# A two-layer encoder on one core: float32r products of 256 and 258 columns read their moving operand from two runs in turn

## The chip, the core and the metric

The kernel runs on one core of a Trainium2 chip, in one launch. TensorE (PE in the profile; its weight loads are PEld) multiplies, VectorE (DVE), ScalarE (ACT) and GpSimd (POOL) do the rest, and SyncE (SP) issues every DMA. The metric is the device time of a run in microseconds, the median of several runs, and lower is better. Before the change it is 2642.24 us (three runs, 2641.88 to 2644.44).

## The reference

Two layers work on 256 tokens of 2048 features in float32. Each layer has a mixer (two attentions, their gates, an output projection) and a gated FFN with a convolution of width 3 over the tokens; both read a normed input that is scaled and shifted by vectors made from `c`.

```
for l in range(DEPTH):
    mod = c_act @ ada_w[l] + ada_b[l]
    sh_a, sc_a, gt_a, sh_m, sc_m, gt_m = [t[:, None, :] for t in jnp.split(mod, 6, axis=-1)]
    h = rmsnorm(x, norm_mix[l]) * (1.0 + sc_a) + sh_a
    qa, ka, va, qb, kb, vb, ga, gb = split_cols(h @ w_in[l])
    ...
    ya = window_attention(qa, ka, va, sink_a[l]) @ w_proj_a[l]
    yb = neighbourhood_attention(qb, kb, vb, rel_bias_b[l]) @ w_proj_b[l]
    merged = jax.nn.sigmoid(ga) * ya + jax.nn.sigmoid(gb) * yb
    x = x + gt_a * (merged @ w_out[l])
    h = rmsnorm(x, norm_ffn[l]) * (1.0 + sc_m) + sh_m
    u = depthwise_conv(h @ w_up[l], conv_w[l], conv_b[l])
    g, v = jnp.split(u, 2, axis=-1)
    x = x + gt_m * ((jax.nn.silu(g) * v) @ w_down[l])
```

## The kernel before

**Numbers in two halves.** PE multiplies float32r operands. To keep float32's precision, every operand is split into a high part (what float32r keeps) and a low part (the rest), and each product of 128x128 weights with its input becomes three: high by high, high by low, low by high.

**The weight stream.** All weights of a layer stand in one sequence of 128x128 blocks (`block_stream`), 16 blocks to a unit of 1 MB. A DMA brings a unit into `w`; ACT copies each half of it as the high part (line 346) and DVE subtracts it from the original for the low part (line 347), both into a tile `hl`. PE takes the blocks in the order of the sequence. The order of the program is that of the code; a background list (`Paced`) puts the steps of the attention, of the norms and of the modulation vectors (a 2048-long DVE product per vector, line 246) between the units.

**Two kinds of products.** `tokens` (lines 427 to 429, for q, k and v) keeps 128 tokens of `h` as the weights of PE and streams 512 columns of `hl`. It already reads them from two runs of 256 in turn: column 0 of the first run, column 0 of the second, column 1 of the first, and so on. Its result stands in PSUM in the same turn, and its readers take every second column. `features` (through `feature_block`, lines 363 to 365) keeps a block of `hl` as the weights and streams the 256 tokens of one chunk of 128 features: `h`, `merged`, the heads' outputs `oA` and `oB`, or the FFN's activations `act`. It reads them as one run. The two attentions do the same on a smaller scale: lines 673 (scores, in float32r for layer 1) and 711 (values).

**258 columns.** While the norm of `x` is still being made, the first columns of the next matrix are multiplied with the input without its norm (class `Bare`): a chunk holds 256 tokens and two more columns, the high and low part of the shift vector, and `level` (line 588) scales the result afterwards.

**Who reads the results.** Lines 998, 1003 and 451 (gates), 455 (gating), 1050 (residual), 588 (level), 676 (scores), 713 and 714 (values) and 1075 and 1077 (the convolution, which takes tokens with their neighbours) read PSUM columns as they stand. `normed` (lines 518 to 522) writes `h`, for the mixer (w = 0) and the FFN (w = 1) alike.

**Places.** `OFF` and `ROW` (48 and 64 elements) shift tiles against each other: most moving operands of `features` begin 192 bytes after a multiple of 256 bytes as counted from the weights of `hl`; the first chunk of a tile may begin at a multiple of 256.

Of the kernel before, what the change touches and what calls it, by code (L numbers as in the profile page):

```python
# [143 lines left out]
def encoder(ctx: ExitStack, tc: tile.TileContext, a: dict, out: bass.AP):  # L144
# [207 lines left out]
    def unit(l, u):  # L352
# [4 lines left out]
        return halves  # L357

    def feature_block(ps, hl, j, act, first, last):

        hi, lo = hl[:, 0, j * P : (j + 1) * P], hl[:, 1, j * P : (j + 1) * P]
        out = ps[:, : act[0].shape[-1]]
        nc.tensor.matmul(out, hi, act[0], start=first, stop=False)  # L363
        nc.tensor.matmul(ps[:, :S], hi, act[1], start=False, stop=False)  # L364
        nc.tensor.matmul(out, lo, act[0], start=False, stop=last)  # L365

    class Stream:
# [32 lines left out]

        def features(self, acts, evacs, late=None, at={}):
# [12 lines left out]
            for ps, evac in zip(pss, evacs):  # L414
                evac(ps[:, : S if not isinstance(acts[0], tuple) else S + 2])

        def tokens(self, h, kcs):

            pss = [mm.tile([P, 512], F32, name=f"ps{self.l}_{self.u}_t{t}", tag="mm") for t in range(2)]
            for kc in kcs:  # L420
                for _ in range(4):
                    hl, j = self.next_block()
                j -= 3
                hi, lo = (hl[:, i, j * P : (j + 4) * P].rearrange("p (a s) -> p s a", a=2) for i in range(2))
                for t, ps in enumerate(pss):
                    xh, xl = (h[kc][:, i, t * P : (t + 1) * P] for i in range(2))
                    nc.tensor.matmul(ps[:], xh, hi, start=kc == kcs[0], stop=False)  # L427
                    nc.tensor.matmul(ps[:], xh, lo, start=False, stop=False)  # L428
                    nc.tensor.matmul(ps[:], xl, hi, start=False, stop=kc == kcs[-1])  # L429
# [4 lines left out]
            return [ps[:].rearrange("p (s a) -> p a s", a=2) for ps in pss]  # L434

# [76 lines left out]
    def normed(l, w, h, rbs):  # L512

        mod, amod = mods[l], amods[l]
        for kc in range(KC):
# [4 lines left out]
            )  # L520
            nc.scalar.activation(out=h[kc][:, 0], in_=t[:], func=AF.Identity, bias=sh)  # L521
            nc.vector.scalar_tensor_tensor(  # L522
                out=h[kc][:, 1], in0=t[:], scalar=sh, in1=h[kc][:, 0].bitcast(F32), op0=ALU.add, op1=ALU.subtract
            )
# [7 lines left out]
    class Bare:  # L532
# [4 lines left out]
        def __init__(self, l, w, sums):  # L537
# [7 lines left out]
            for tag in homes + ["qn"]:  # L545
# [3 lines left out]
                for i in range(k):  # L549

                    off = 2 * self.half * i + (0 if self.chunks else ROW - OFF)
                    c = t[:, off : off + 2 * self.half].rearrange("p (a s) -> p a s", a=2)
                    self.chunks.append((c[:, 0, : S + 2], c[:, 1, :S]))
            assert len(self.chunks) == KC

        def add(self, kc):
            need(self.l, 48 * self.w + 2 * kc + 2)
            c, scale = self.chunks[kc], amods[self.l][:, self.w, kc : kc + 1]
            sh = mods[self.l][:, 3 * self.w * KC + kc : 3 * self.w * KC + kc + 1]
            hi, lo = c  # L560
            nc.scalar.activation(out=hi[:, :S], in_=x[:, kc], func=AF.Identity, scale=scale)
            nc.vector.scalar_tensor_tensor(
                out=lo, in0=x[:, kc], scalar=scale, in1=hi[:, :S].bitcast(F32), op0=ALU.mult, op1=ALU.subtract
            )
# [18 lines left out]
        def level(self, ps, scale=1.0):  # L583
# [3 lines left out]
            nc.scalar.activation(out=sh[:, 1:], in_=ps[:, S : S + 2], func=AF.Copy, scale=scale, accum_out=sh[:, :1])  # L587
            nc.vector.tensor_tensor(out=z[:], in0=ps[:, :S], in1=self.rbs[:], op=ALU.mult)
            return z, sh
# [78 lines left out]
    def attend(q, k, v, p, mask, scale, sink, o, rows=None):  # L668

        sc = ax.tile([P, 2, S], F32, name="sc", tag="ax")  # L670
        for t in range(2):
            for i, j in by(q):
                nc.tensor.matmul(sc[:, t], q[i][:, t * P : (t + 1) * P], k[j], start=i + j == 0, stop=(i, j) == by(q)[-1])  # L673
        m = sm.tile([P, 2], F32, name="m", tag="m")
        for t in range(2):
            nc.vector.tensor_tensor_reduce(
                out=p[:, t], in0=sc[:, t], in1=mask[:, t], scale=scale, scalar=-3.0e38 if sink is None else sink,
                op0=ALU.add, op1=ALU.max, accum_out=m[:, t : t + 1],
# [30 lines left out]
        for i, j in by(v):  # L709
            for b in range(2):  # L710
                nc.tensor.matmul(po[:, :S], v[i][:, b], pT[:, j, b], start=i + j + b == 0, stop=i + b == 2)  # L711
        o = o()
        nc.scalar.copy(o[:, 0], po[:, :S])
        nc.vector.tensor_tensor(out=o[:, 1], in0=po[:, :S], in1=o[:, 0].bitcast(F32), op=ALU.subtract)

# [120 lines left out]
    for l in range(L):  # L836
# [117 lines left out]
        for pi, (groups, gates) in enumerate(parts):  # L954
# [38 lines left out]
            for mo in range(BARE[0] if l else 0, KC):  # L993

                def gate_a(ps):
                    src = ps
                    if pi > 0:
                        nc.vector.tensor_tensor(out=ya[:, mo], in0=ps, in1=ya[:, mo], op=ALU.add)  # L998
                        src = ya[:, mo]
                    if last:  # L1000
                        half_tanh(ya[:, mo], src)
                    elif pi == 0:
                        nc.scalar.copy(ya[:, mo], ps)

# [6 lines left out]
        for mo in range(KC):  # L1011

            def proj_a(ps):
                gated(ya[:, mo], ya[:, mo], ps)

# [11 lines left out]
        def gate_b(mo):  # L1027
            def evac(ps):
                half_tanh(gb[mo], ps)

# [6 lines left out]
        for mo in range(KC):  # L1037

            def merge(ps):
                z = ev.tile([P, S], F32, name="m", tag="z")  # L1040
                gated(z[:], gb[mo], ps)
                nc.vector.tensor_tensor(out=z[:], in0=z[:], in1=ya[:, mo], op=ALU.add)
# [38 lines left out]
        for gi, chunks in enumerate(FF_GROUPS):  # L1081
# [34 lines left out]
            for cs in sets:  # L1116
# [4 lines left out]
                else:  # L1121
                    for fn in fns:
                        st.features(src, [fn])
                if gi == 0 and cs[-1] == BARE[1] // 2 - 1:
# [107 lines left out]
```

## Time and profile before

| | before |
|---|---|
| median of 3 runs | 2642.24 us |
| the profiled execution, its own time | 2642.45 us |
| its span (first to last instruction) | 2640.7 us |
| granted TensorE clock, mean | 0.999 |
| HBM read, written | 695.06 MB, 2.10 MB |

The span is what the trace covers; 1.75 us lie around it. PE works nearly the whole span. A PE row's length is longer than the distance to the next one, since products overlap in the array: what counts for the time is the distance from start to start, which the lists in order of time and the counts by stretch give.

```profile
PE   8999999999999999999999999999999999999999
DVE  8998998997987888788887778869888776655664
ACT  5445865456643554355555666555575445544553
DMA  9998689885777777777766656677757775555554
```

These are busy tenths in 40 equal slices of 66 us. The products of `tokens` lie in the first five slices (layer 0) and in slices 22 to 24 (layer 1); all the rest is `features` and the attention.

### The profile page before, as it was taken

What the parts mean: (1) busy time and instruction counts of PE and PEld (TensorE: products, weight loads), DVE (VectorE), ACT (ScalarE), POOL (GpSimd) and SP (SyncE); (2) the same over time, 40 slices, a digit from 0 to 9 for tenths busy, and PEclk for the clock granted to TensorE, in tenths of its full rate; (3) what the DMA queues carried; (4) which work ended last, traced back from release to release, by engine and by line L of the source; (5) the groups of instructions that cost most, each with busy time, mean ns of one, the idle gap of its engine ahead of it and who ended that gap; (6) DMA issues with size and microseconds to landing.
All of it is one profiled execution on the core that took longest, in us unless ns stands there. A gap on an engine that the chain in (4) does not pass through costs nothing.

```text
span 2640.7 us, 51000 instructions
## 1 busy us (share of the span) xinstructions
PE 2619.6 (99%) x21164; PEld 2555.7 (97%) x21164; DVE 2120.1 (80%) x2979; ACT 1405.9 (53%) x2280; POOL 247.6 (9%) x345
## 2 busy tenths in 40 slices
PE   8999999999999999999999999999999999999999
PEld 6999899999999999999998889999999999999999
DVE  8998998997987888788887778869888776655664
ACT  5445865456643554355555666555575445544553
POOL 0001100000000000000003658620000000000000
PEclk9999999999999999999999999999999999999999
DMA  9998689885777777777766656677757775555554
GB/s 369 352 348 297 251 316 343 317 326 199 287 288 288 299 291 290 293 288 290 295 224 260 255 210 254 247 269 269 278 181 278 287 262 194 195 199 193 192 192 144
DMA packets 102185, 700.45 MB, mean 265 GB/s; under 512 B 12865, under 2 KB 15169, under 8 KB 18113
## 3 DMA queue, kind: packets, MB, share of 16 engines
q1 hardware_dynamic: 101954, 697.20, 71.1%
q8 instruction: 165, 2.70, 0.4%
q14 instruction: 66, 0.54, 0.1%
HBM read 695.06 MB, written 2.10 MB: 264 GB/s over the span
## 4 chain that ended last, share of the span: by engine, by line
PE 85%; DVE 6%; DMA 3%; POOL 3%; ACT 2%; issue 2%; SPq 0%; POOLq 0%; DVEq 0%; ACTq 0%
PE ps L363 26%; PE ps L365 25%; PE ps L364 25%; PE ps_t L428 2%; PE ps_t L427 2%; PE ps_t L429 2%; DVE hl L347 2%; DMA aw<-in_aw 2%; DVE aw L246 2%; POOL packA L318 1%; POOL p L318 1%; DMA w<-in_ws 1%; ACT hl L346 1%; PE sc L673 1%; PE po L711 1%
## 5 line engine op out<-in xcount | busy, mean ns | idle before, releaser
L347 DVE TENSOR_TENSOR hl<-w,hl 128x1024 fp32r<-128x1024 f32 x928 | 1132.6, 1226 | 325.2 <-ACT hl L346 321.2
L346 ACT CAST hl<-w 128x1024 fp32r<-128x1024 f32 x928 | 969.5, 1049 | 718.9 <-PE ps L365 505.5
L363 PE MATMUL ps<-h,hl 128*128 128x256 f32 x3328 | 922.2, 277 | 1.3 <-DVE ya L998 0.6
L364 PE MATMUL ps<-h,hl 128*128 128x256 f32 x3328 | 919.2, 276 | 0.0
L365 PE MATMUL ps<-h,hl 128*128 128x256 f32 x3328 | 919.0, 276 | 0.0
L363 PEld LDWEIGHTS ps<-h,hl 128*128 128x128 f32 x3328 | 624.7, 188 | 2.4 <-DVE ya L998 0.8
L364 PEld LDWEIGHTS ps<-h,hl 128*128 128x128 f32 x3328 | 624.8, 188 | 0.4 <-DVE h L522 0.2
L365 PEld LDWEIGHTS ps<-h,hl 128*128 128x128 f32 x3328 | 624.3, 188 | 0.0
L246 DVE CUSTOM_DVE_ANT_0 aw<-aw,cact,ab 128x2048 f32<-128x2048 f32 x189 | 443.7, 2348 | 12.3 <-DMA aw<-in_aw 12.2
L427 PE MATMUL ps_t<-hl,h 128*128 128x512 f32 x576 | 217.4, 382 | 4.3 <-ACT h L521 2.7
L1077 DVE SCALAR_TENSOR_TENSOR u<-ps,cw,u 128x255 f32<-128x255 f32 x304 | 146.2, 481 | 92.9 <-ACT u L1075 88.5
L428 PE MATMUL ps_t<-hl,h 128*128 128x512 f32 x576 | 219.6, 382 | 1.1 <-DVE hl L347 0.9
L429 PE MATMUL ps_t<-hl,h 128*128 128x512 f32 x576 | 218.6, 380 | 0.0
L1075 ACT ACTIVATE u<-ps,cw 128x256 f32<-128x256 f32 x152 | 85.7, 564 | 214.8 <-PE ps L365 214.7
L365 PE MATMUL ps<-merged,hl 128*128 128x256 f32 x512 | 141.7, 277 | 0.5 <-DVE hl L347 0.5
L364 PE MATMUL ps<-merged,hl 128*128 128x256 f32 x512 | 141.5, 277 | 0.0
L363 PE MATMUL ps<-merged,hl 128*128 128x256 f32 x512 | 141.5, 277 | 0.0
L364 PE MATMUL ps<-act_o,hl 128*128 128x256 f32 x512 | 141.3, 276 | 0.0
L365 PE MATMUL ps<-act_o,hl 128*128 128x256 f32 x512 | 141.3, 276 | 0.0
L363 PE MATMUL ps<-act_o,hl 128*128 128x256 f32 x512 | 141.0, 276 | 0.0
L427 PEld LDWEIGHTS ps_t<-hl,h 128*128 128x128 f32 x576 | 108.9, 190 | 20.9 <-ACT h L521 3.7
L428 PEld LDWEIGHTS ps_t<-hl,h 128*128 128x128 f32 x576 | 109.2, 190 | 18.1 <-DVE hl L347 3.2
(244 smaller groups left out, 4817.1 us busy)
## 6 DMA issues: line engine op xcount, KB each, us to landing
w<-in_ws SPq DMA_DIRECT2D x463, 1024.0 KB, 4.9
aw<-in_aw SPq DMA_DIRECT2D x189, 1024.0 KB, 5.5
p<-in_bias SPq DMA_DIRECT2D x16, 256.0 KB, 4.5
x<-in_xT SPq DMA_DIRECT2D x4, 512.0 KB, 5.5
aw_o<-in_aw SPq DMA_DIRECT2D x2, 1024.0 KB, 12.4
out<-x SPq DMA_DIRECT2D x16, 128.0 KB, 2.5
w<-in_ws SPq DMA_DIRECT2D x2, 512.0 KB, 11.7
aw_b<-in_aw SPq DMA_DIRECT2D x1, 1024.0 KB, 18.2
```

The costliest lines, as they stand in the source:

```text
L246: product = nc.vector.tensor_tensor_reduce(out=raw[:], in0=raw[:], in1=cact[:], scale=1.0, scalar=ab[:, i : i + 1], op0=ALU.mult, op1=ALU. ...
L318: nc.gpsimd.tensor_copy(out=dst[a : a + BLOCK, :, :, b : b + BLOCK], in_=src[b : b + BLOCK, :, :, a : a + BLOCK])
L346: nc.scalar.copy(hl[:, 0], r)
L347: nc.vector.tensor_tensor(out=hl[:, 1], in0=r, in1=hl[:, 0].bitcast(F32), op=ALU.subtract)
L363: nc.tensor.matmul(out, hi, act[0], start=first, stop=False)
L364: nc.tensor.matmul(ps[:, :S], hi, act[1], start=False, stop=False)
L365: nc.tensor.matmul(out, lo, act[0], start=False, stop=last)
L427: nc.tensor.matmul(ps[:], xh, hi, start=kc == kcs[0], stop=False)
L428: nc.tensor.matmul(ps[:], xh, lo, start=False, stop=False)
L429: nc.tensor.matmul(ps[:], xl, hi, start=False, stop=kc == kcs[-1])
L1075: nc.scalar.activation(out=u, in_=ps, func=AF.Identity, scale=w[:, 1:2], bias=w[:, 3:4])
L1077: nc.vector.scalar_tensor_tensor(out=u[:, to], in0=ps[:, of], scalar=w[:, j : j + 1], in1=u[:, to], op0=ALU.mult, op1=ALU.add)
```

## The change

All float32r products of 256 and 258 columns now read the moving operand from two runs in turn, as `tokens` did: columns 0, 128, 1, 129 and so on (0, 129, 1, 130 with 258). The number of columns, of products and of weight loads stays, and each product still writes its columns of PSUM one after another, so PSUM holds tokens 0, 128, 1, 129. Readers take every second column, and write two runs of 128. A chunk of 258 puts the two columns of the shift behind each run. The FFN's `h` is stored turned instead (even tokens in the first run, odd ones in the second), so that its product comes out in the order of the tokens and the convolution reads PSUM as before (`sorted=True`). The float32 scores of layer 0 (one term, `len(q) == 1`) stay as they were.

```
+    def turns(columns):
+        return columns.rearrange("p (r q) -> p q r", r=2)
+    def turned_back(columns):
+        return columns.rearrange("p (q r) -> p r q", r=2)
+    def pair(columns):
+        return columns.rearrange("p (r q) -> p r q", r=2)
...
     def feature_block(ps, hl, j, act, first, last):
-        out = ps[:, : act[0].shape[-1]]
+        out = ps[:, : 2 * act[0].shape[1]]
...
-                    feature_block(ps, hl, j, (act[:, 0], act[:, 1]) if not isinstance(act, tuple) else act, i == 0, i == len(acts) - 1)
+                    act_of = act if isinstance(act, tuple) else (turns(act[:, 0]), turns(act[:, 1]))
+                    feature_block(ps, hl, j, act_of, i == 0, i == len(acts) - 1)
...
-                evac(ps[:, : S if not isinstance(acts[0], tuple) else S + 2])
+                evac(ps[:, : S + 2] if isinstance(acts[0], tuple) else ps[:, :S] if sorted else turned_back(ps[:, :S]))
...
+            hi, lo, src = h[kc][:, 0], h[kc][:, 1], t[:]
+            if w:
+                hi, lo, src = turns(hi), turns(lo), src.rearrange("p (q r) -> p q r", r=2)
-            nc.scalar.activation(out=h[kc][:, 0], in_=t[:], func=AF.Identity, bias=sh)
+            nc.scalar.activation(out=hi, in_=src, func=AF.Identity, bias=sh)
...
-                    self.chunks.append((c[:, 0, : S + 2], c[:, 1, :S]))
+                    self.chunks.append((turns(c[:, 0, : S + 2]), turns(c[:, 1, :S])))
...
-            nc.scalar.copy(hi[:, S : S + 1], sh)
-            nc.vector.tensor_tensor(out=hi[:, S + 1 :], in0=sh, in1=hi[:, S : S + 1].bitcast(F32), op=ALU.subtract)
+            src, first, second = pair(x[:, kc]), hi[:, 0, P:], hi[:, 1, P:]
+            nc.scalar.copy(first, sh)
+            nc.vector.tensor_tensor(out=second, in0=sh, in1=first.bitcast(F32), op=ALU.subtract)
...
-                nc.tensor.matmul(po[:, :S], v[i][:, b], pT[:, j, b], start=i + j + b == 0, stop=i + b == 2)
+                nc.tensor.matmul(po[:, :S], v[i][:, b], turns(pT[:, j, b]), start=i + j + b == 0, stop=i + b == 2)
...
-            nc.vector.scalar_tensor_tensor(out=x[:, mo], in0=ps, scalar=gt, in1=x[:, mo], op0=ALU.mult, op1=ALU.add)
+            to = pair(x[:, mo])
+            nc.vector.scalar_tensor_tensor(out=to, in0=ps, scalar=gt, in1=to, op0=ALU.mult, op1=ALU.add)
```

PE, POOL and SP keep their instructions in the same order, and every tile keeps its address. 109 more waits stand on PE, each for one of its own products that lies at least 20 products back. On ACT and DVE one thing moves: the copies of the shift (128x1) for the last chunks of a `Bare` set now stand behind the chunk's own write instead of up to a dozen units ahead of it. First ACT, at the end of layer 0's output projection (`bare_1_y` are chunks of the FFN's unnormed input, `hl_99` and `hl_100` weight units). Before:

```order
L561 ACTIVATE bare_1_y_5621<-x,amod_177 128x256
L346 CAST hl_99_0_6635<-w_99_6633 128x1024
L346 CAST hl_99_1_6638<-w_99_6633 128x1024
L473 ACTIVATE sq<-x 128x256
L561 ACTIVATE bare_1_y_5622<-x,amod_177 128x256
L346 CAST hl_100_0_6643<-w_100_6641 128x1024
```

and after, at the same place:

```order
L578 ACTIVATE bare_1_y_5621<-x,amod_177 128x2x128
L346 CAST hl_99_0_6635<-w_99_6633 128x1024
L582 CAST bare_1_y_5621<-mod_172 128x1
L346 CAST hl_99_1_6638<-w_99_6633 128x1024
L486 ACTIVATE sq<-x 128x256
L578 ACTIVATE bare_1_y_5622<-x,amod_177 128x2x128
L346 CAST hl_100_0_6643<-w_100_6641 128x1024
L582 CAST bare_1_y_5622<-mod_172 128x1
```

The 128x1 copy of each chunk now comes one weight copy after the chunk. On DVE at the same place, where the second shift column is made, before:

```order
L562 SCALAR_TENSOR_TENSOR bare_1_y_5621<-x,amod_177,bare_1_y_5621 128x256
L347 TENSOR_TENSOR hl_99_0_6635<-w_99_6633,hl_99_0_6635 128x1024
L1050 SCALAR_TENSOR_TENSOR x<-ps_97_16_0_6499,mod_172,x 128x256
L347 TENSOR_TENSOR hl_99_1_6638<-w_99_6633,hl_99_1_6638 128x1024
L475 TENSOR_TENSOR sqa<-sqa,sq 128x256
```

and after:

```order
L579 SCALAR_TENSOR_TENSOR bare_1_y_5621<-x,amod_177,bare_1_y_5621 128x256
L347 TENSOR_TENSOR hl_99_0_6635<-w_99_6633,hl_99_0_6635 128x1024
L583 TENSOR_TENSOR bare_1_y_5621<-mod_172,bare_1_y_5621 128x1
L1071 SCALAR_TENSOR_TENSOR x<-ps_97_16_0_6499,mod_172,x 128x256
L347 TENSOR_TENSOR hl_99_1_6638<-w_99_6633,hl_99_1_6638 128x1024
```

Here too one 128x1 subtraction has moved in ahead of the residual's read of PSUM.

More of the change, by code (lines that the diff above doesn't have):

```diff
@@ L399, in next_block, with features @@
             return self.halves[j // 8], j % 8
-        def features(self, acts, evacs, late=None, at={}):
+        def features(self, acts, evacs, late=None, at={}, sorted=False):
             pss = [mm.tile([P, 512], F32, name=f"ps{self.l}_{self.u}_{self.at}_{m}", tag="mm") for m in range(len(evacs))]
@@ L423, in tokens @@
                 j -= 3
-                hi, lo = (hl[:, i, j * P : (j + 4) * P].rearrange("p (a s) -> p s a", a=2) for i in range(2))
+                hi, lo = (turns(hl[:, i, j * P : (j + 4) * P]) for i in range(2))
                 for t, ps in enumerate(pss):
@@ L433, in tokens @@
                     self.tick()
-            return [ps[:].rearrange("p (s a) -> p a s", a=2) for ps in pss]
+            return [turned_back(ps[:]) for ps in pss]
     def split(dst, src, scale=None, held=False):
@@ L587, in level @@
             nc.scalar.activation(out=sh[:, 1:], in_=ps[:, S : S + 2], func=AF.Copy, scale=scale, accum_out=sh[:, :1])
[L588 removed]
+            nc.vector.tensor_tensor(out=pair(z[:]), in0=turned_back(ps[:, :S]), in1=pair(self.rbs[:]), op=ALU.mult)
             return z, sh
@@ L672, in attend @@
             for i, j in by(q):
-                nc.tensor.matmul(sc[:, t], q[i][:, t * P : (t + 1) * P], k[j], start=i + j == 0, stop=(i, j) == by(q)[-1])
+                key = turns(k[j]) if len(q) > 1 else k[j]
+                nc.tensor.matmul(sc[:, t], q[i][:, t * P : (t + 1) * P], key, start=i + j == 0, stop=(i, j) == by(q)[-1])
         m = sm.tile([P, 2], F32, name="m", tag="m")
@@ L1122, in encoder @@
                     for fn in fns:
-                        st.features(src, [fn])
+                        st.features(src, [fn], sorted=True)
                 if gi == 0 and cs[-1] == BARE[1] // 2 - 1:
```

32 lines of the change are left out of this document (17 added, 15 removed).

## The prediction

> **What bounds the kernel now.** I read the page first: its busy times, then its chain of work that ended last.
>
> ```profile
> PE 2619.6 (99%) x21164; PEld 2555.7 (97%) x21164; DVE 2120.1 (80%) x2979; ACT 1405.9 (53%) x2280; POOL 247.6 (9%) x345
> PE 85%; DVE 6%; DMA 3%; POOL 3%; ACT 2%; issue 2%; SPq 0%; POOLq 0%; DVEq 0%; ACTq 0%
> PE ps L363 26%; PE ps L365 25%; PE ps L364 25%; PE ps_t L428 2%; PE ps_t L427 2%; PE ps_t L429 2%; DVE hl L347 2%; DMA aw<-in_aw 2%; DVE aw L246 2%; POOL packA L318 1%; POOL p L318 1%; DMA w<-in_ws 1%; ACT hl L346 1%; PE sc L673 1%; PE po L711 1%
> ```
>
> Three lines of PE, those of `feature_block`, hold 76% of the chain. Next I looked where other engines set the end, in a table by stretches (us, then the busy time of PE, PEld, DVE, ACT, POOL with their instructions, the granted clock, the DMA share, GB/s):
>
> ```profile
> 0.00:330.00 330.00, 317.19 (x1860) 281.41 (x1861) 301.04 (x431) 187.33 (x363) 22.24 (x15) 1.00 0.86 324
> 330.00:396.00 66.00, 66.00 (x540) 64.30 (x540) 63.68 (x119) 40.83 (x85) 0.00 (x0) 1.00 0.85 316
> 396.00:1385.00 989.00, 988.53 (x8630) 987.28 (x8630) 840.71 (x1155) 513.65 (x775) 2.32 (x2) 1.00 0.77 288
> 1385.00:1600.00 215.00, 210.53 (x1051) 186.13 (x1051) 159.03 (x233) 129.82 (x279) 120.16 (x167) 0.98 0.65 245
> 1600.00:2636.00 1036.00, 1036.00 (x9080) 1035.48 (x9080) 755.19 (x1042) 534.22 (x782) 102.91 (x161) 1.00 0.62 227
> ```
>
> The third and the fifth stretch are nearly all products of 256 and 258 columns, and PE has no gap: 989 us for 8630 products is 114.6 ns each, 1036 us for 9080 is 114.1 ns. The clock is granted in full, so neither waits nor throttling explain the pace. Up to 330 us and around 1500 us lie the 512-column products; at 330 to 396 us DVE works 63.68 of 66 us and PE needs 122 ns for an instruction, so DVE sets the pace there.
>
> What is one product's pace made of? Lists in order of time, first and last row of each group (start, length, line): 55 rows of 256 columns in one run, 34 rows of 512 columns in two runs, 53 rows of `Bare`, mixed 258 and 256.
>
> ```profile
> 1079.77 0.28 PE L365 MATMUL ps<-act_b,hl 128*128 128x256 f32 x1
> ...
> 1085.89 0.28 PE L365 MATMUL ps<-act_b,hl 128*128 128x256 f32 x1
> ```
> ```profile
> 1463.78 0.38 PE L428 MATMUL ps_t<-hl,h 128*128 128x512 f32 x1
> ...
> 1470.90 0.38 PE L428 MATMUL ps_t<-hl,h 128*128 128x512 f32 x1
> ```
> ```profile
> 1929.77 0.28 PE L365 MATMUL ps<-bare_b,hl 128*128 128x258 f32 x1
> ...
> 1935.95 0.28 PE L363 MATMUL ps<-bare_qn,hl 128*128 128x258 f32 x1
> ```
>
> From start to start: 6.12 us over 54 steps, 113.3 ns; 7.12 over 33, 215.8 ns; 6.18 over 52, 118.8 ns. Half of 215.8 is 107.9 ns: columns that come from two runs stream faster than one run of 256, though the two-run products have a weight load beside them too. With two more columns the pace falls by 5.5 ns, far more than two columns' share, 0.8 ns. So the one-run stream loses time to something that depends on timing, and I take it for a clash of its reads with those of the weight load. A run of 256 columns covers 1024 bytes in the time in which the load covers 512, so it overtakes the load; two runs of 128 walk 512 bytes each, at the load's own pace. That is my reading; no row shows a clash itself.
>
> The other bound is the weight load. [...]
>
> ```profile
> 13.54 2.76 PEld L462 LDWEIGHTS warm<-ident 128*128 128x128 f32 x24
> 619.08 0.19 PEld L365 LDWEIGHTS ps<-bare_a,hl 128*128 128x128 f32 x1
> ...
> 619.19 0.19 PEld L363 LDWEIGHTS ps<-bare_a,hl 128*128 128x128 f32 x1
> ```
>
> 24 loads of the warming products (4-byte weights, 128 columns) take 2.76 us, less the last one's 0.19: 2.57 over 23 steps, 111.7 ns. The float32r load at 619.08, which follows a product of one column and has no long stream beside it, is followed by the next after 0.11 us. So loads one behind the other need about 111.7 ns, whatever streams.
>
> **The change part by part.** *The reading.* It removes no product; it changes the pace of 6272 + 6272 + 6272 (lines 363 to 365), 192 (line 711) and 96 (line 673), 19,104 in all. From below the new pace is bound by half the two-run product, 107.9 ns, and by the load's 111.7 ns; from above by the present mixed pace of 118.8 ns, should a clash remain. I take **111.7 ns**, the nearest row, since it has the same load beside a stream that covers 512 bytes in a product, as each run will. Does the load itself survive beside two runs?
>
> ```profile
> L428 PEld LDWEIGHTS ps_t<-hl,h 128*128 128x128 f32 x576 | 109.2, 190 | 18.1 <-DVE hl L347 3.2
> L364 PEld LDWEIGHTS ps<-h,hl 128*128 128x128 f32 x3328 | 624.8, 188 | 0.4 <-DVE h L522 0.2
> L482 PEld LDWEIGHTS ssm<-mean,sq 128*128 128x128 f32 x8 | 1.1, 192 | 0.0
> ```
>
> Beside a two-run stream it lasts 190 ns, beside one run 188, beside a product of one column 192: the two runs don't stretch it.
>
> The sum by stretches: 989 - 8630 x 0.1117 = 25.0 us and 1036 - 9080 x 0.1117 = 21.8 us, together **47 us**. The few transposes and score products in these counts are priced alike, a small error. From the 1,600 or so further one-run products (before 396 us and around 1500 us) I count nothing: DVE and the DMAs are late next there (DMA share 0.86 up to 330 us). If they gained as much, 2.6 ns each, it would be 4 us. In the two long stretches DVE, 840.71 us in 989, would go to 87% of the shorter time and the DMA share from 0.77 to 0.79: neither becomes the bound on average.
>
> A rule of the Trainium skill speaks against this. In "SBUF — State Buffer", section "Door 1: The DMA port swizzle", it says that accesses which stay in a 16-byte line get the full bandwidth and that each one which crosses to a new line pays; with two runs in turn every column is in another line than the last. The trace gives no sign of such a price at 512 columns, where two runs take 215.8 ns, less than twice 113.3; a row of 512 float32r columns in one run is not there to compare. What it would do to the time stands with the last rival.
>
> *The readers.* Readers of PSUM with every second column are in the trace already, next to plain ones:
>
> ```profile
> L968 DVE TENSOR_TENSOR packB<-ps_t,packB 128x512 f32<-128x512 f32 x24 | 15.7, 681 | 0.0
> L998 DVE TENSOR_TENSOR ya<-ps,ya 128x256 f32<-128x256 f32 x32 | 13.0, 416 | 3.4 <-PE ps L365 3.4
> L966 ACT COPY packB<-ps_t 128x512 f32<-128x512 f32 x12 | 6.7, 585 | 5.4 <-PE ps_t L429 5.2
> L1003 ACT COPY ya<-ps 128x256 f32<-128x256 f32 x16 | 5.8, 370 | 12.2 <-PE ps L365 12.2
> L347 DVE TENSOR_TENSOR hl<-w,hl 128x1024 fp32r<-128x1024 f32 x928 | 1132.6, 1226 | 325.2 <-ACT hl L346 321.2
> L346 ACT CAST hl<-w 128x1024 fp32r<-128x1024 f32 x928 | 969.5, 1049 | 718.9 <-PE ps L365 505.5
> ```
>
> From a plain read of 256 columns to one of 512 with the stride DVE needs 265 ns more (1.04 a column), from 256 to the 1024 plain columns of line 347 810 ns more (1.05). ACT's steps are 215 ns (0.84) and 679 (0.88). So the stride has no price: 0, and in the long stretches both engines have idle time that would hide a small one.
>
> *The FFN's `h`, stored turned.* 32 writes on ACT and 32 on DVE put neighbours 512 bytes apart. No row shows that. Bounds: nothing, or as much again as the whole instruction, 479 ns on DVE (line 522): 32 x 0.48 = 15 us, half for each layer, in a stretch where DVE has about a seventh of its time free and the first products that need this `h` come only after the `Bare` set. I take 0; uncovered it would be up to 15 us.
>
> *What moves.* Nine pairs of 128x1 copies stand later on ACT and DVE, and nothing is removed or doubled; the chunks they complete are read by PE after more weight units. Cost 0; three pairs in a row at the end, uncovered, are under 1 us. *The new waits.* PE's 109 waits are for its own products 20 or more back, which is over 2 us ago: always met. Behind a waiting product stands the rest of PE, but it would not stop.
>
> The sum stands against the profiled execution's own time, 2642.45 us, 0.2 us above the median 2642.24: 2642.45 - 47 = 2595.4, so **2595 us**.
>
> **The rivals.**
>
> *The load hides and the stream alone counts.* For it: float32r loads show 188 to 190 ns against the 192 of float32's, so their own pace may lie below 111.7. Against: the step of 0.11 us after one-column products. Midway between 107.9 and 111.7, at 109.8 ns, 989 - 947.6 and 1036 - 997.0 give 80 us: 2562; at 107.9 it is 114 us, 2528. "TensorE: Matmul & The Clock Gate" in the Trainium skill (section "Back-to-back issue gap") has columns / 2.4 + 2.5 ns, thus 109.2 ns for 256, and that would be an estimate of 2551; at 512 columns its 215.8 is what the trace has.
>
> *The pace stays.* 113.3 ns would be what a float32r load needs beside any stream, or the change doesn't touch what slows the stream. For it: 113.3 is only 1.6 above the loads' own pace. Then at best the irregular products come down to it: 989 - 978.0 and 1036 - 1029.0 make 18 us, 2624; or nothing, 2642.
>
> *Slower: the turn costs more line reads.* Each column then opens another place in the memory than the column before, and a load that shares the pace of both runs may meet them all the time instead of in passing, above all where first chunks lie at the weights' own offset. It decides in every `features` product, from a mean pace above the present 114.3 ns. Priced at the irregular pace of today, 118.8 ns: 17,710 products x 118.8 = 2104 us against 2025, 79 us more, 2721. Against it: the three load rows and the 512-column pace. At its worst each column costs double. The nearest row for that is the float32 score product, whose rows of 256 columns last as long as those of 512 float32r columns:
>
> ```profile
> 1463.99 0.38 PE L429 MATMUL ps_t<-hl,h 128*128 128x512 f32 x1
> L673 PE MATMUL sc<-packA 128*128 128x256 f32 x32 | 9.4, 380 | 0.0
> ```
>
> Both last 380 ns, so I price it at the 512 columns' pace: 17,710 x (215.8 - 114.3) adds 1.8 ms. The line rule of the Trainium skill cited above is of this kind, without a figure. I give that end 0.02 of the chance of slower.
>
> **How the numbers follow.** The forecast (a pace of 110.8 to 112.5, 2580 to 2612 us) 0.58; the stream alone 0.13; the pace stays 0.14, of which 0.05 with a gain that can be told; slower 0.15. Faster is 0.58 + 0.13 + 0.05 = 0.76, same 0.09, slower 0.15; 0.2%, some 5 us, is about what a measurement of this kernel can tell from no change. The range leaves out the slower rival and the end of the second: 2540 to 2645.
>
> **What would show it.** The stretches of plain products should hold 590 or 591 products in 66 us (583 to 585 now), and the products of `Bare` should keep the same pace as the others, no longer 118.8. The matmul rows of 256 columns should last some 274 ns instead of 276. Unchanged DVE and ACT means at lines 1050, 455 and 451 would bear out the readers. A pace that stays at 113.3 in the long stretches, longer load rows than 192 ns, or a DVE that is busy without gaps while PE waits would each prove a step wrong.

## The result, and the profile after

The changed kernel takes 2605.79 us, the median of four runs (2603.60 to 2608.11), beside 2642.14 us for the kernel before in four runs. The ratio is 0.9861 with a 95% interval of 0.9844 to 0.9878: 36 us faster, where 47 had been forecast (2595 us). Its profiled execution took 2603.6 us, the lowest of the four, with a span of 2601.8 us: 38.9 us less than the span of before.

The page of the kernel after, first the busy times and then the chain of work that ended last, by engine and by line:

```profile
PE 2574.4 (99%) x21164; PEld 2507.9 (96%) x21164; DVE 2122.7 (82%) x2979; ACT 1404.2 (54%) x2280; POOL 247.9 (10%) x345
PE 78%; DVE 9%; DMA 4%; ACT 3%; POOL 3%; issue 3%; SPq 0%; DVEq 0%; POOLq 0%; ACTq 0%
PE ps L377 23%; PE ps L375 23%; PE ps L376 23%; DVE hl L347 3%; DMA aw<-in_aw 3%; PE ps_t L440 2%; PE ps_t L441 2%; PE ps_t L442 2%; DVE aw L246 2%; ACT hl L346 1%; POOL packA L318 1%; POOL p L318 1%; DMA w<-in_ws 1%; PE sc L691 1%; POOL qrs L506 1%
```

DVE's work is nearly the same (2120.1 us before), but PE's share of the chain has fallen from 85% to 78%, and DVE's and the DMAs' have grown from 9% to 13% together. PE is still busy 99% of the span, yet it now waits for others in places where it did not. The table by stretches of the kernel after has the same products in each row as that of before (the borders are the starts of the same products; columns as there):

```profile
0.00:329.20 329.20, 316.31 (x1860) 280.05 (x1861) 301.13 (x431) 187.25 (x363) 22.25 (x15) 0.99 0.86 324
329.20:393.80 64.60, 64.48 (x541) 62.51 (x541) 62.07 (x119) 39.24 (x81) 0.00 (x0) 1.00 0.84 315
393.80:1365.10 971.30, 967.79 (x8631) 965.13 (x8630) 843.77 (x1155) 514.30 (x778) 2.32 (x2) 1.00 0.79 294
1365.10:1579.30 214.20, 209.25 (x1051) 184.86 (x1050) 159.02 (x233) 129.51 (x279) 120.37 (x167) 0.99 0.66 246
1579.30:2595.70 1016.40, 1015.33 (x9081) 1014.26 (x9081) 756.23 (x1042) 533.92 (x783) 102.94 (x161) 1.00 0.64 231
```

Row by row, against before: 0.8 us less, 1.4 less, **17.7 less** (forecast 25.0), 0.8 less, **19.6 less** (forecast 21.8). Behind the last row 6.1 us are left, where before had 4.7: 1.4 us more. Together that is the 38.9 us.

The pace itself is in the lists in order of time: first and last row of 55 plain products of 256 columns, and of 58 products of `Bare`, both of the kernel after.

```profile
1060.80 0.28 PE L375 MATMUL ps<-act_b,hl 128*128 128x256 f32 x1
...
1066.83 0.28 PE L375 MATMUL ps<-act_b,hl 128*128 128x256 f32 x1
...
1901.95 0.27 PE L376 MATMUL ps<-bare_b,hl 128*128 128x256 f32 x1
...
1908.32 0.27 PE L376 MATMUL ps<-bare_qn,hl 128*128 128x256 f32 x1
```

6.03 us over 54 steps are 111.7 ns, and 6.37 us over 57 steps are 111.8 ns: plain products and `Bare` now have the same pace, that of the load. The groups of lines 375 and 376 say the same in another way:

```profile
L375 PE MATMUL ps<-h,hl 128*128 128x256 f32 x3328 | 916.1, 275 | 1.9 <-DVE ri L709 0.8
L376 PEld LDWEIGHTS ps<-h,hl 128*128 128x128 f32 x3328 | 638.9, 192 | 0.4 <-DVE h L538 0.2
```

A product lasts 275 ns (277 at this place before), a load 192 instead of 188: no longer than beside a product of one column (192). A window of 66 us, in the FFN of layer 1, of before and then of after (counts include the rows that lap over an edge):

```profile
2400.00:2466.00 66.00, 66.00 (x583) 66.00 (x582) 39.91 (x49) 31.39 (x39) 0.00 (x0) 1.00 0.54 192
```
```profile
2400.00:2466.00 66.00, 66.00 (x593) 66.00 (x592) 45.89 (x63) 35.38 (x50) 0.00 (x0) 1.00 0.55 193
```

Readers of every second column of PSUM, in the kernel after:

```profile
L1018 DVE TENSOR_TENSOR ya<-ps,ya 128x256 f32<-128x256 f32 x32 | 13.0, 417 | 2.6 <-PE ps L377 2.6
L1023 ACT COPY ya<-ps 128x256 f32<-128x256 f32 x16 | 5.8, 370 | 11.5 <-PE ps L377 11.5
L1071 DVE SCALAR_TENSOR_TENSOR x<-ps,mod,x 128x256 f32<-128x256 f32 x128 | 60.0, 479 | 19.7 <-PE ps L377 19.2
```

With the columns read in a row these had 416, 370 and 478 ns. The stride costs a reader nothing.

The writers of the FFN's `h`, stored turned, are another matter. Length of one (smallest, median, largest ns) on DVE in layer 0, before and then after, and last on ACT after:

```profile
L522 DVE SCALAR_TENSOR_TENSOR h<-ht,mod,h x16: 478/482/486, 629.1 to 679.5; 128x256 fp32r<-128x256 f32 x16
```
```profile
L538 DVE SCALAR_TENSOR_TENSOR h<-ht,mod,h x16: 667/690/709, 623.9 to 674.7; 128x256 fp32r<-128x256 f32 x16
```
```profile
L537 ACT ACTIVATE h<-ht,mod x16: 713/752/776, 623.1 to 673.2; 128x256 fp32r<-128x256 f32 x16
```

For 256 columns with neighbours 512 bytes apart DVE needs 208 ns more; its instruction also reads one operand, the high part, in that order. ACT only writes so. The group of all its 64 writes, before and then after:

```profile
L521 ACT ACTIVATE h<-ht,mod 128x256 fp32r<-128x256 f32 x64 | 30.4, 501 | 32.1 <-DVE ht L518 31.8
```
```profile
L537 ACT ACTIVATE h<-ht,mod 128x256 fp32r<-128x256 f32 x64 | 37.2, 626 | 33.9 <-DVE ht L531 33.5
```

Half of them are turned: about 250 ns more for each turned write. By length that is 6.7 us more on DVE (32 x 0.208) and 8.0 on ACT. Neighbouring rows overlap a little: by busy time the groups grew by 6.8 us on ACT (30.4 to 37.2) and by 6.2 on DVE (29.5 to 35.7). The turned writes lie in the stretch of `Bare` (610 to 680 us, and again in layer 1).

### The profile page after: what moved, and what is told of

It is laid out like the page before. It is cut to its first block, busy times and chain, and to the rows that moved or that the text cites. A ratio compares the mean times of both kernels' runs of the same rounds, so it can differ in the third digit from the quotient of the medians.

```text
span 2601.8 us, 51007 instructions
## 1 busy us (share of the span) xinstructions
PE 2574.4 (99%) x21164; PEld 2507.9 (96%) x21164; DVE 2122.7 (82%) x2979; ACT 1404.2 (54%) x2280; POOL 247.9 (10%) x345
## 4 chain that ended last, share of the span: by engine, by line
PE 78%; DVE 9%; DMA 4%; ACT 3%; POOL 3%; issue 3%; SPq 0%; DVEq 0%; POOLq 0%; ACTq 0%
PE ps L377 23%; PE ps L375 23%; PE ps L376 23%; DVE hl L347 3%; DMA aw<-in_aw 3%; PE ps_t L440 2%; PE ps_t L441 2%; PE ps_t L442 2%; DVE aw L246 2%; ACT hl L346 1%; POOL packA L318 1%; POOL p L318 1%; DMA w<-in_ws 1%; PE sc L691 1%; POOL qrs L506 1%
## 5 line engine op out<-in xcount | busy, mean ns | idle before, releaser
L375 PEld LDWEIGHTS ps<-h,hl 128*128 128x128 f32 x3328 | 638.8, 192 | 3.1 <-ACT hl L346 0.9
L376 PEld LDWEIGHTS ps<-h,hl 128*128 128x128 f32 x3328 | 638.9, 192 | 0.4 <-DVE h L538 0.2
L377 PEld LDWEIGHTS ps<-h,hl 128*128 128x128 f32 x3328 | 638.6, 192 | 0.0
L246 DVE CUSTOM_DVE_ANT_0 aw<-aw,cact,ab 128x2048 f32<-128x2048 f32 x189 | 444.0, 2350 | 12.1 <-DMA aw<-in_aw 11.7
L1096 ACT ACTIVATE u<-ps,cw 128x256 f32<-128x256 f32 x152 | 85.8, 564 | 198.6 <-PE ps L377 198.6
```

The source lines that it names most:

```text
L246: product = nc.vector.tensor_tensor_reduce(out=raw[:], in0=raw[:], in1=cact[:], scale=1.0, scalar=ab[:, i : i + 1], op0=ALU.mult, op1=ALU. ...
L1096: nc.scalar.activation(out=u, in_=ps, func=AF.Identity, scale=w[:, 1:2], bias=w[:, 3:4])
```

## The experiments

Two questions were open: what makes the pace 111.7 ns with two runs and more with one, and who took the missing 10 us.

**Shorter streams.** In after (`narrow_two`) and in before (`narrow_one`, as one run) the second and third product of each block read 192 of their columns. The edit in after:

```
+NARROW = 192
...
-        nc.tensor.matmul(ps[:, :S], hi, act[1], start=False, stop=False)
-        nc.tensor.matmul(out, lo, act[0], start=False, stop=last)
+        nc.tensor.matmul(ps[:, :NARROW], hi, act[1][:, : NARROW // 2], start=False, stop=False)
+        nc.tensor.matmul(ps[:, :NARROW], lo, act[0][:, : NARROW // 2], start=False, stop=last)
```

> The changed kernel with the second and third product of each block of features cut from 256 (258) to 192 columns; it leaves out the two correcting products for 64 of the 256 tokens. Theory L (loading weights, 111.7 ns each, sets the new pace): the pace stays at 111.7 ns, 590 to 592 products in 66 us, time 2600 to 2610 us. Rival S (the stream sets it): two of three products shrink to three quarters, near 84 ns, the mean to 93, and some 300 us go, until VectorE is the bound: 2250 to 2350 us.

> The kernel before with the same cut to 192 columns, read as one run; it leaves out the two correcting products for 64 of the 256 tokens. Theory C1 (beside a weight load the one-run stream is stretched, the load itself is not): the narrow products have room to spare and take the load's 111.7 ns, the 256-column ones keep 113 to 119; mean near 112.5 ns, time 2605 to 2618 us. Rival C2 (the load is stretched by the stream): all products stay at 113.3 ns or more, 2628 to 2645 us.

Measured: 2910.76 and 2938.82 us. Both times are far above every expectation, but the pace can be read where PE doesn't wait. PE's rows of `narrow_two` in order of time:

```profile
2400.13 0.25 PE L377 MATMUL ps<-act_o,hl 128*128 128x192 f32 x1
2400.21 0.28 PE L378 MATMUL ps<-act_o,hl 128*128 128x192 f32 x1
2400.32 0.30 PE L376 MATMUL ps<-act_o,hl 128*128 128x256 f32 x1
2400.46 0.25 PE L377 MATMUL ps<-act_o,hl 128*128 128x192 f32 x1
```

The steps differ, but three products take 0.33 us, as many as with 256 columns (3 x 111.7 = 335 ns): a sixth of the columns is gone and not a nanosecond is won. So the weight load sets the pace of after, and the shorter streams gained nothing here.

A window of 66 us from 2400 us on holds 594 products in `narrow_two`. In `narrow_one` it is

```profile
2400.00:2466.00 66.00, 66.00 (x584) 66.00 (x584) 48.78 (x53) 28.12 (x31) 0.00 (x0) 1.00 0.76 288
```

The products that start there are 113.4 ns apart on average, and three take 340 ns, 5 more than in two runs. So one run keeps the extra of all three products, though two of them have 64 columns to spare. The mean is that of theory C2 (the load is stretched), but 4 of the 5 ns lie in the step behind the 256-column product, as C1 has it. Whether the stream or the load is stretched stays open.

The times rose for another reason. What DVE waited for, and a window in layer 0, of `narrow_two`:

```profile
DVE aw L247 <- DMA aw<-in_aw: 238.3, 65, 6.8
```
```profile
540.00:612.00 72.00, 47.71 (x316) 46.26 (x315) 33.13 (x43) 21.62 (x35) 0.00 (x0) 0.74 0.52 194
```

DVE waits 238 us for the loads of the modulation vectors (11.7 us idle for that reason in after), PE stands a third of the window, and its granted clock is 0.74 there. With narrower products the order of the work on ACT, DVE and SP is not that of after either, so these two times say nothing on the change; the circle behind such waits comes up again below.

**Other ways to turn.** In two kernels made from after, `features` reads its 256 columns from four runs of 64 in turn (`four_runs`), or the even columns and then the odd ones (`evens_odds`).

```
...
-                    act_of = act if isinstance(act, tuple) else (turns(act[:, 0]), turns(act[:, 1]))
+                    act_of = act if isinstance(act, tuple) else tuple(act[:, i].rearrange("p (r q) -> p q r", r=4) for i in range(2))
```
```
...
+                    act_of = act if isinstance(act, tuple) else tuple(act[:, i].rearrange("p (q r) -> p r q", r=2) for i in range(2))
```

> The changed kernel, but products of 256 columns read four runs of 64 in turn, and their results come out with the tokens in another order (readers are not adapted). Theory P (a clash is avoided because each run walks through the memory at the load's own pace): four runs walk at half the load's pace, which passes them, so the pace is irregular again, 113 to 119 ns, 2630 to 2720 us. Rival R (taking columns from far places in turn is enough): 111.7 ns, 2600 to 2610 us.

> The changed kernel, but products of 256 columns read all even columns of one run and then all odd ones (readers are not adapted, tokens come out in another order). Theory P: the stream walks four times as fast as the load and passes it twice, so the pace is that of before or worse, 113 to 119 ns, 2635 to 2720 us. Rival R needs places far apart in turn and expects 113.3 ns as well, 2635 to 2645 us. Rival Q (fewer of the columns of a 16-byte piece in a row is what helps): 111.7 ns, 2600 to 2610 us.

Measured: 3133.98 and 4623.3 us. Windows of 66 us without a wait, of `four_runs` and then of `evens_odds`:

```profile
2700.00:2766.00 66.00, 66.00 (x464) 66.00 (x463) 32.63 (x42) 26.32 (x34) 0.00 (x0) 1.00 0.45 160
```
```profile
4000.00:4066.00 66.00, 66.00 (x290) 59.80 (x289) 18.60 (x21) 13.31 (x14) 0.00 (x0) 1.00 0.28 96
```

From start to start it is 143 and 229 ns: no theory had such sizes. Neither kernel is held by the load's pace (111.7 ns); the stream itself is slower. In "SBUF — State Buffer" of the Trainium skill, section "Door 1: The DMA port swizzle", two hits in each 16-byte line are enough for the full bandwidth and a new line for each access pays. Here every second column in a row, which hits each line twice, takes twice as long (229 ns). Two runs in turn, which change the line with every column, pay nothing (111.7 ns), while four, which change it as often, do pay (143 ns). So these runs don't bear the rule out for this stream.

**How near the two runs lie.** `four_runs` differs from after in the number of runs and in their distance, 256 bytes instead of 512. `two_near` has two runs at 256 bytes:

```
...
+                    act_of = act if isinstance(act, tuple) else tuple(act[:, i].rearrange("p (h r q) -> p h q r", h=2, r=2) for i in range(2))
```

> After's feature products read two runs in turn that begin 256 bytes apart (each half of 128 columns as two runs of 64 in turn) in place of 512 bytes apart; the Bare and token products stay as in after. The columns arrive in another order than their readers take, so the output isn't the reference's. What made the run with four runs of 64 columns take 143 ns per product? Theory N (number of runs: a third and fourth run cost, two are free at any distance): 111.7 ns, 2600 to 2610 us. Theory D (distance: 256 bytes is too near): 125 to 145 ns, 2820 to 3140 us.

Measured: 2602.01 us in one run, and the window has as many products as after's:

```profile
2400.00:2466.00 66.00, 66.00 (x594) 66.00 (x592) 45.88 (x63) 35.38 (x50) 0.00 (x0) 1.00 0.55 193
```

Theory N: whether two runs lie 256 or 512 bytes apart doesn't matter; that there are four does.

**Where the operands lie.** The pads between the tiles taken out of after (`flat_two`) and of before (`flat_one`), so that moving operand and weights begin at the same place:

```
-OFF, ROW = 48, 64
+OFF, ROW = 0, 0
```

> After's kernel with the two pads taken out of the activations' places (OFF and ROW 0 in place of 48 and 64 words), so that nearly every moving operand begins at the same place, modulo 1 KB, as the weights. The sums are unchanged and so is the order of the instructions on every engine. Theory P (two runs meet no clash, whatever their place): pace 111.7 ns as in after, 2600 to 2610 us. Rival (the gain of two runs needs these places too): 113 to 120 ns per product, 2630 to 2760 us.

> Before's kernel with the same two pads taken out: one run, at the weights' own place. Theory P (one run clashes with the load's reads, by its place): the pace of all products becomes that of the one chunk that lies so in before (113 to 119 ns, mean near 116): 19,100 products by 2 to 3.5 ns more than 114.1, so 2675 to 2710 us. Rival (the place doesn't matter, one run is slow by itself): 114.1 ns and 2642 us as before.

Measured: 2603.86 us for two runs, 2749.22 us for one. The same window, `flat_two` and then `flat_one`:

```profile
2400.00:2466.00 66.00, 66.00 (x593) 66.00 (x593) 45.88 (x63) 35.55 (x49) 0.00 (x0) 1.00 0.54 196
```
```profile
2400.00:2466.00 66.00, 66.00 (x552) 66.00 (x551) 36.84 (x46) 27.71 (x33) 0.00 (x0) 1.00 0.52 178
```

Two runs keep 111.6 ns (mean of the 19,013 steps up to 160 ns behind products of 256 and 258 columns); one run goes from 114.2 to 119.9 ns, all over the kernel, with nothing changed but addresses. So how long a one-run product takes depends on where its operands lie, and a two-run product shows no such dependence. Theory P holds, though its price was low (119.9 instead of 116). The edit shifts operands and weights against each other and also in memory as a whole; which of the two counts wasn't separated.

**One run of 512 columns.** In after, `tokens` alone goes back to one run.

```
-                hi, lo = (turns(hl[:, i, j * P : (j + 4) * P]) for i in range(2))
+                hi, lo = (hl[:, i, j * P : (j + 4) * P] for i in range(2))
...
-            return [turned_back(ps[:]) for ps in pss]
+            return [pair(ps[:]) for ps in pss]
```

> After's kernel with the token products (1,728 of 512 columns, at 215.9 ns in before and after, which both read two runs in turn) put back to one run; its readers take the columns plainly. Theory C (one run clashes only while a weight load of 128 columns runs beside it): 4 ns more per product at most, as the 256-column product lost (113.3 ns against its 109 of stream): 218 to 220 ns, 2608 to 2614 us by 1,700 of them where waits don't take it. Rival R (a one-run stream is slower over its whole length): twice that per product, 222 to 226 ns, 2615 to 2623 us. Rival 0 (512 columns hide it): 215.9 ns, no change.

Measured: 2609.41 us. First and last of 37 rows of `tokens_one`:

```profile
1439.64 0.39 PE L442 MATMUL ps_t<-hl,h 128*128 128x512 f32 x1
...
1447.80 0.39 PE L442 MATMUL ps_t<-hl,h 128*128 128x512 f32 x1
```

8.16 us over 36 steps are 226.7 ns; the mean of all 1,679 steps up to 250 ns is 228.1, against 215.9 in two runs: 12.2 ns for each product, more than either theory had. The time, 5.6 us above that of `flat_two`, would fit theory C, but it can't decide: it is one run, runs of after alone lie between 2600 and 2609 us, and of the 20.5 us that 1,679 x 12.2 ns would make, most is hidden where `tokens` waits anyway.

By the kernel's addresses, nine in ten of these products (1566 of 1728) have moving operand and weights at the same place modulo 256 bytes, as in `flat_one`, where one run of 256 columns lost 119.9 - 107.9 = 12.0 ns on half of 215.8. There the 512-column product loses as much, once and not twice, which would speak for C's mechanism. The other tenth, 192 bytes apart like most products of 256 columns in before, speaks against it. Six of them in a row in `tokens_one` start with the first of these rows and end where the second starts:

```profile
1458.22 0.40 PE L440 MATMUL ps_t<-hl,h 128*128 128x512 f32 x1
...
1459.62 0.39 PE L440 MATMUL ps_t<-hl,h 128*128 128x512 f32 x1
```

1.40 us over six steps are 233 ns, 17 more than in two runs. A product of 256 columns lost 113.3 - 107.9 = 5.4 ns at that place. So here twice the length loses three times as much, and the place that is the better one for 256 columns is the worse one for 512. Neither C nor R holds as stated; how the loss goes with length and place stays open.

**DVE's work in the out-projection of layer 0.** In after this stretch was no shorter than before (88.4 and 88.6 us), with DVE busy for 92% of it. Before and then after:

```profile
527.30:615.70 88.40, 87.94 (x770) 87.75 (x769) 80.19 (x125) 46.01 (x77) 0.00 (x0) 1.00 0.85 315
```
```profile
522.20:610.80 88.60, 86.86 (x771) 86.10 (x770) 81.85 (x128) 46.47 (x77) 0.00 (x0) 1.00 0.86 315
```

Three kernels side by side: after itself (`after_again`), 30 additions given to POOL (`pool_adds`), the same 30 left out (`no_adds`). The edits of the second are

```
+             self.eng = nc.gpsimd if name == "ssm0" else nc.vector
-                nc.vector.tensor_tensor(out=self.acc[:], in0=self.acc[:], in1=sq[:], op=ALU.add)
+                self.eng.tensor_tensor(out=self.acc[:], in0=self.acc[:], in1=sq[:], op=ALU.add)
...
-                nc.vector.tensor_tensor(out=z[:], in0=z[:], in1=ya[:, mo], op=ALU.add)
+                (nc.vector if l else nc.gpsimd).tensor_tensor(out=z[:], in0=z[:], in1=ya[:, mo], op=ALU.add)
```

and the third has these two statements under a condition that leaves layer 0 out.

> After's kernel unchanged, as the measure for the two runs beside it: 2602 to 2609 us.

> After's kernel with 30 additions of 128x256 in layer 0 (the 16 that add the branches' merge, the 14 that add up squares behind the out-projection; 0.42 us each on DVE) given from DVE to POOL, which has 0.70 us of work between 522 and 680 us. Theory W (in these 158 us of after's profile DVE is 90% busy and late, so that the faster pace gives nothing there): some 12 us of DVE's work less, PE waits 2 to 3 us less, 2600 to 2604 us where the unchanged kernel of the same call has 2605. Rival (the weights' DMA or ACT ends last there, or POOL is too slow to hand the sums over in time): no change within 0.1%, or 2 to 5 us more.

> After's kernel with the same 30 additions of layer 0 left out altogether (so its output isn't the reference's): the most that giving them away can bring. Theory W: 2599 to 2603 us, 2 to 6 less than the unchanged kernel. Rival (DVE isn't what is late): the same as the unchanged kernel within 2 us.

Measured: 2604.62 us (ratio to before 0.9839 to 0.9872), 2617.99 us (0.9893 to 0.9923) and 2604.94 us (0.9839 to 0.9868). Theory W falls: without the additions nothing is won. The four runs of each kernel spread over 6 to 8 us, so the times alone could not tell the 2 us that W had at least; but the stretch itself is no shorter either, 90.1 us beside 89.8 in `after_again`. The stretch of `no_adds`, and what DVE waits for most in it:

```profile
522.00:612.10 90.10, 87.27 (x771) 86.19 (x770) 74.64 (x105) 45.85 (x76) 0.00 (x0) 1.00 0.84 308
```
```profile
DVE aw L246 <- DMA aw<-in_aw: 8.8, 7, 2.4
```

In the same stretch of `after_again` DVE waits 4.2 us for these loads. DVE has some 7 us less to do (74.64 us beside 81.97) and spends more than half of it on waiting for the loads of the modulation vectors. Its rows show the circle. Chain of waits of `no_adds` between 562 and 582 us (start, us, what; the first row is the share by line):

```profile
by line: DMA aw<-in_aw 59.8%; issue 33.2%; DVE hl L347 11.4%; DVE bare_b L580 2.0%; DVE x L1073 2.0%; DVE mod L246 1.4%; DVE aw L246 0.4%; DVE amod L255 0.3%; DVEq L347 0.1%
...
562.29 4.84 DMA aw<-in_aw
...
569.54 7.11 DMA aw<-in_aw
```

The load at 562.29 is issued 0.02 us after DVE's product of the vector before, which frees one of the four 1 MB buffers; it lands 4.84 us later, and DVE takes it at once. The next, at 569.54, again follows that product and takes 7.11 us. Splits of weights (line 347) stand behind these products on DVE. A DVE with less to do waits longer for the next load (8.8 us beside 4.2).

`pool_adds` is worse for a reason of its own: POOL needs 1.26 us for one such addition where DVE needs 0.42, and PE waits for the merge. Groups of POOL and waits of PE in its out-projection stretch:

```profile
L489 POOL TENSOR_TENSOR sqa<-sqa,sq 128x256 f32<-128x256 f32 x13 | 16.3, 1257 | 59.5 <-ACT sq L487 59.4
```
```profile
PE ps L375 <- DVE m L468: 5.2, 2, 2.8
```

**Fewer loads.** After without 16 of the modulation vectors of layer 0:

```
+LEFT_OUT = range(64, 80)
...
         for n, i in enumerate(ADA_ORDER):
+            if l == 0 and n in LEFT_OUT:
+                nc.vector.memset(mod[:, i : i + 1], 1.0)
...
+                done[l] = n + 1
+                yield
+                continue
```

> After's kernel without 16 of the modulation vectors of layer 0 (numbers 64 to 79 in their order: their 1 MB loads, which share four buffers with the weight units, and DVE's product of 2.35 us each; the values are set to 1 instead, so the output isn't the reference's). In no_adds DVE's extra free time went into waiting for these loads: each is issued when DVE frees a buffer, lands 5 to 7 us later, and DVE's next split of weights stands behind it. Theory B (that circle of load, DVE and buffer is what is late in the out-projection of layer 0): PE's steps of over 160 ns there, 2.4 to 3.7 us in excess before, fall below 1 us; those of the Bare set behind it (2.7 us, behind ACT's and DVE's convolution and norm) stay; 2 to 4 us less than the 2604.6 of the unchanged kernel, so 2600 to 2603 us. Rival (the steps come from ACT, or from the merge's own latency): they stay above 2 us, and the time within 1 us of 2604.6.

Measured: 2600.00 us in five runs (2599.51 to 2600.75; ratio to before 0.9826 to 0.9853). The same products as above, the out-projection and then `Bare`, of `fewer_loads`:

```profile
521.90:607.70 85.80, 85.80 (x771) 85.80 (x770) 58.53 (x90) 44.83 (x69) 0.00 (x0) 1.00 0.56 197
607.70:676.50 68.80, 67.23 (x589) 65.96 (x588) 60.15 (x106) 51.53 (x100) 0.70 (x1) 1.00 0.53 184
```

PE has no gap left in the out-projection (85.8 of 85.8 us, 2.8 less than after), and `Bare` behind it is what it was (68.8 us): theory B, in both halves. So the circle of load, DVE's product and shared buffer holds PE up there. Which part of it does isn't shown: with each load the edit also takes DVE's product of 2.35 us, and DVE has 23 us less to do in this stretch (58.53 us beside 81.85), three times what `no_adds` took. That DVE spent the time won in `no_adds` on waiting for loads speaks for the loads; their transfer and their place in the queue weren't separated either.

## Why the prediction was right, and where its size was off

**The pace.** Forecast 111.7 ns, measured 111.7 in plain products and 111.8 in `Bare`. The load as the bound was right: `narrow_two` shortens streams and three products still take 0.33 us. The rival in which the stream alone counts is out by the same run. That the pace stays is out by the result. The rival of more line reads doesn't occur with two runs, but it wasn't empty: with four runs it is 143 ns. That chance stood for something real.

**The reason.** That one run loses time which two runs in turn don't is borne out: addresses alone move its pace from 114.2 to 119.9 ns, and two runs are free of that at both places (`flat_one`, `flat_two`). The prediction compared 512 columns in two runs with 256 in one; 512 in one run are now there too, and half of 226.7 is 113.4 ns, so the difference came from the turns and not from the length. That the weight load is what the stream clashes with is still argued and not shown: no run took the load away. Nor is the place modulo 256 bytes the whole account, since most products of `Bare` in before lie 192 bytes off like the plain ones and took 118.8 ns where those took 113.3. The picture behind it, two runs that walk at the load's own pace, fits `two_near` (its runs walk so too) but was not tested by itself.

**The sum.** This is the term that was mis-sized: 989 - 8630 x 0.1117 and 1036 - 9080 x 0.1117 counted everything over 111.7 ns as pace that would go, and no new wait. Starts of PE's rows, matched one to one between the two traces, divide it (excess over 111.67 ns):

| | forecast | steps up to 160 ns gained | longer steps, before | longer steps, after | net |
|---|---|---|---|---|---|
| 396 to 1385 us | 25.0 | 22.5 us | 26 with 3.5 us | 40 with 8.3 us | 17.7 us |
| 1600 to 2636 us | 21.8 | 21.5 us | 8 with 0.9 us | 14 with 2.7 us | 19.7 us |

(With the rounded borders of the table by stretches the last is 19.6.)

The pace gave 44.0 of the forecast 46.8 us; the rest of that sum were waits that before had already (3.5 and 0.9 us; roundings make the difference). New waits then took 6.6 us. 2.1 of them lie in the out-projection of layer 0 (0.7 to 2.8 us), in the circle that `fewer_loads` breaks up; 2.5 and 1.8 us lie in the two `Bare` stretches behind the out-projections (0.9 to 3.5 and 0.9 to 2.7). "Neither becomes the bound on average" was true, 87% for DVE and 0.79 for the DMAs as forecast, and it was the wrong question: a mean over 970 us hides the 160 us in which others are late. (At the slow end of the forecast pace, 112.5 ns, the prediction's own sum gives 2610 us and not 2612.)

**What wasn't counted.** The stretches that were priced at nothing gave 3.0 us (0.8, 1.4 and 0.8); the end behind PE's last product took back 1.4. 2.5 us more lie between this execution (38.9 us) and the medians (36.4).

**The readers** cost 0, as said: 417 and 370 ns against 416 and 370. **The FFN's `h`** was taken at 0, and that step failed: 0.21 us for each write on DVE and about 0.25 on ACT, some 13 us of busy time in all. It lies in the `Bare` stretches, beside 4.3 us of new waits of PE. In layer 0's (616 to 686 us before, 611 to 680 after) weight loads now wait longer for the low parts that DVE makes (line 347), before and then after:

```profile
PEld ps L365 <- DVE hl L347: 0.2, 1, 0.2
```
```profile
PEld ps L377 <- DVE hl L347: 1.6, 3, 0.7
```

These splits stand on DVE among the writes of `h`. How much of the waits those writes made, and how much is only that PE comes sooner, wasn't tried.

**The moved copies** are met by waits on other engines: in after ACT stands 2.9 us in all before three of them, for DVE's write of the same chunk, and DVE 0.5 us before two. PE's list of waits names neither a moved copy nor a product of its own; one weight load, at 318 us, stands 0.9 us behind a product, where before it stood 0.8 us for DVE.

## What to carry to other kernels

Where a product streams about as long as its weight load takes, look at the distance from start to start: if it is longer than both the load's own step and the columns' share, try two runs in turn, or other addresses, before anything else, and measure before taking more than two runs: four cost more here than two save. When a gain in pace is summed, sum only the steps without a wait, and look in each stretch for the engine or the load that has just a few per cent to spare: it takes its part back. A writer that scatters neighbours may cost half as much again (501 to about 750 ns on ACT), even where a reader's stride in PSUM is free.

## What the hardware showed unexpectedly

256 float32r columns take 111.7 ns in two runs (the load's pace), 113.3 or 119.9 in one run with nothing changed but addresses, 143 in four runs of 64, and 229 as even and odd columns. 512 columns take 215.9 ns in two runs and about 227 or 233 in one, and there the other place is the better one. Writes into SBUF with neighbours 512 bytes apart took 690 instead of 482 ns on DVE (which also read one operand so) and 752 on ACT, while every second column of PSUM was read at the plain pace. An addition of 128x256 took 1.26 us on POOL and 0.42 on DVE.
